# GpSimd's large elementwise work to VectorE, and a planner's matmul cost set to the traced spacing

## The chip, the cores and the metric

The kernel runs on one core of a Trainium2 chip. The metric is the device time of one execution in microseconds (us). TensorE does the products, ScalarE, VectorE and GpSimd the elementwise work, and SyncE (SP) issues the loads.

## The reference, cut to what matters

Two transformer blocks on 256 tokens of 1024 features, in 32-bit floats, one after the other:

```
x = x + 0.5 * rms_norm(swiglu(rms_norm(x)))            # ffn1
x = x + rms_norm(mixer1(rms_norm(x)))                  # windowed attention, window means
x = x + 0.5 * rms_norm(swiglu(rms_norm(x)))            # ffn2
x = x + concat(ssd(u), mla(u)) @ w_out_2               # second mixer: recurrence and latent attention
x = x + memory_attention(rmsnorm(x), rmsnorm(mem))
x = x + conv_ffn(rmsnorm(x))                           # taps along the tokens
return rmsnorm(x)
```

The feed-forward width is 2816; every weight is used once for the 256 tokens.

## The kernel before

**Split products.** To keep 32-bit accuracy each operand is split in two parts of a shorter format: `hi` is the rounded value, `lo` the rest. A product is three matmuls, `hi*hi + hi*lo + lo*hi`, summed in one bank of PSUM (`mm3`, `mm2`, `projB`). The other products (transposes, scores, recurrence) are in plain 32-bit floats.

**Weights.** `wblock` (L660) loads up to 1024 columns on 128 partitions into one of four `raw` tiles, ScalarE copies them into `hi`, and a subtraction gives `lo`. The raw tile is free again when the subtraction has ended. Which engine subtracts is set in `sub` (L600): always VectorE in the phases "start", "ffn" and "cffn", VectorE or GpSimd in "mix" (first mixer) and "mix2" (second mixer and the attention over the memory), by the table `POOL_LO` (L30).

**Products of two tiles.** `mul` (L597) may run on VectorE or GpSimd in every phase. It scales the attention weights (`softmax_p` with `norm`), makes the decays and scaled inputs of the recurrence (`ssd_rec`), the scaled tokens (`Into.done`) and the last gains (`Final.half`).

**Small work.** The norms' power of -0.5 on one column is always on GpSimd (`rsq`, `rstd`). `copy` and `scale` may run on ScalarE or VectorE.

**Order.** `Plan` records every instruction with its tiles, its allowed engines and an estimated time (`Plan.cost`, L280). `Plan.schedule` (L304) is a list schedule: again and again it takes, of all engines, the instruction that can start first, with the earlier recorded one first among equals. Where two engines are allowed, one that would finish later than the other has the difference added to its start. Tiles get slots, and a load or write waits for a slot. The instructions are then issued in the order of their planned starts (L470 issues all, so the profile gives this line for nearly everything). On each engine that order is fixed: an instruction that has to wait holds all that follow it on its engine.

The estimates in question:

```
if dt == F32R:                                                        # L288
    return 2.5 + (n / 2.4 if n >= 256 else 4 * n / 2.4)               # one matmul of n columns, ns
...
return (0.52 if one else 1.04) * size(out) + (130 if ps else 70)      # VectorE
return 1.05 * size(out) * (2 if out.tile.dtype == F32R else 1) + 464  # GpSimd
```

For 1024 columns with the split's output type the planner puts a subtraction at 1135 ns on VectorE and 2614 ns on GpSimd. It has no cost for one engine slowing another.

Of the kernel before, what the change touches and what calls it, by code (L numbers as in the profile page):

```python
# [9 lines left out]
F32 = mybir.dt.float32  # L10
# [4 lines left out]
ALU = mybir.AluOpType  # L15
# [14 lines left out]
POOL_LO = {"start": 0, "ffn": 0, "mix": 1, "mix2": 1, "cffn": 0}  # L30
# [42 lines left out]
# vectors over features, a chunk of 128 to a column; ffn1_pre apart  # L73
# [3 lines left out]
# short vectors, on every partition  # L77
ROWS = ["sinks", "ssd_dt_bias_2", "ssd_a_log_2", "ssd_d_2"]

# weights, cut by columns: first column, width of a block; a block lies by its row in a chunk of 128, then by chunk  # L80
# [9 lines left out]
def layout(inputs):  # L90
    """the arrays in memory: small vectors packed, the others as they are"""
    out = dict(inputs)
    cols = lambda name: np.asarray(out.pop(name)).reshape(-1, P).T
    c = constants()
    out["first"] = cols("ffn1_pre")
    out["cols"] = np.concatenate([cols(n) for n in COLS], axis=1)
    out["rows"] = np.concatenate([np.asarray(out.pop(n)).reshape(1, -1) for n in ROWS], axis=1)
    out["pos"] = np.concatenate([cols("positions"), cols("positions_2")], axis=1)
    out["xT"] = np.asarray(out["x"])[0].reshape(2 * P, KD, P).transpose(2, 1, 0)
    for name, cuts in TILED.items():  # L100
        w = np.asarray(out.pop(name))[0]
        for (c0, n), (c1, _) in zip(cuts, cuts[1:] + [(w.shape[1], 0)]):
            out[f"{name}_from{c0}"] = w[:, c0:c1].reshape(-1, P, (c1 - c0) // n, n).transpose(2, 1, 0, 3)
    return {**out, **c}


class Tile:
    """A tile on chip before it has an address: taken from a class of slots at its first write."""
# [16 lines left out]
class View:  # L125
    """Slices of a tile, kept until the tile has an address; ix tells which columns they touch, rows which partitions."""
# [85 lines left out]
class Plan:  # L212
    """Records the instructions of the program, orders them on their engines by a list schedule that follows
    their data, their slots and their estimated times, and then issues them to Tile in that order."""
# [40 lines left out]
    def access(self, n, v, w):  # L255
        t = v.tile
        if t not in n.tiles:
            assert w or t.acc, ("read before any write", n.label)
            n.tiles.append(t)
            t.left += 1  # L260
        if t.cls == "ps":
            mask, rows = np.ones(1, bool), (0, P)
        else:
            mask, rows = np.zeros(int(np.prod(t.shape[1:])), bool), v.rows
            mask[v.ix[0].ravel()] = True
        keep = []
        for m, ow, omask, orows in t.acc:
            if m is not n:
                hit = rows[0] < orows[1] and orows[0] < rows[1] and (omask & mask).any()
                if hit and (w or ow):  # L270
                    n.deps.add(m)
                # a write that covers an earlier access takes its place
                if w and rows[0] <= orows[0] and orows[1] <= rows[1] and not (omask & ~mask).any():
                    continue
            keep.append((m, ow, omask, orows))
        keep.append((n, w, mask, rows))
        t.acc = keep

    @staticmethod
    def cost(attr, op, a, k):  # L280
        out = k.get("out", a[0] if a else None)
        size = lambda v: int(np.prod(v.shape[1:]))
        ps = any(isinstance(v, View) and v.tile.cls == "ps" for v in list(a) + list(k.values()))
        if attr == "tensor":
            if op == "transpose":
                return 109.0
            n, dt = size(out), k["rhs"].tile.dtype
            if dt == F32R:  # L288
                return 2.5 + (n / 2.4 if n >= 256 else 4 * n / 2.4)
            return 5 + max(n, P) / 2.4 * (4 if dt == F32 else 1)  # L290
        if attr == "sync" or op == "dma_start":
            n = int(np.prod(out.shape)) * 4
# [3 lines left out]
        if attr == "vector":  # L296
            if op == "reduce_max":
                return 1.04 * size(a[1]) + 70
            one = op in ("tensor_copy", "tensor_scalar") and not ps
# [4 lines left out]
    def schedule(self):  # L304
# [9 lines left out]
        known = {e: [] for e in names}  # L314
# [9 lines left out]
        weights = 0  # L324
# [12 lines left out]
        def slot_time(n):  # L337
            """when the slots of the node's new tiles are there; None: not yet known"""
# [5 lines left out]
            for c, ts in need.items():  # L344
# [10 lines left out]
                # the oldest tiles keep the last slots, and none runs far ahead of them  # L355
# [117 lines left out]
class Transposed:  # L473
    """Chunks of 128 features of one tile of tokens, split in two; four chunks of both tiles of tokens to a tile of memory."""
# [13 lines left out]
class Into:  # L488
    """The tokens transposed and split for the products that follow. late: not scaled, their products are; rows: and
    with the scales along the tokens; both: and scaled as well."""  # L490
# [49 lines left out]
class Final:  # L540
    """The last norm, and out."""
# [24 lines left out]
class K:  # L566
# [23 lines left out]
    def transposed(self, nk):  # L590
        """memory for nk chunks of both tiles of tokens"""
        return tuple([self.w1024(F32R) for _ in range(0, nk, 4)] for _ in range(2))
# [4 lines left out]
    def mul(self, out, a, b):  # L597
        self.nc.add([(e, "tensor_tensor", (out, a, b), {"op": ALU.mult}) for e in ("vector", "gpsimd")])

    def sub(self, out, a, b):  # L600
        alts = ["vector"] + ["gpsimd"] * POOL_LO[self.phase]
        self.nc.add([(e, "tensor_sub", (out, a, b), {}) for e in alts])
# [29 lines left out]
    def load_xT(self, k0, k1):  # L632
        """chunks of the tokens as they lie transposed, with their gains, split"""
# [20 lines left out]
    def bc(self, v, ap):  # L654
        """one row on every partition"""
        self.nc.sync.dma_start(v, ap.partition_broadcast(P))
        return v

# [1 line left out]
    def wblock(self, src):  # L660
# [8 lines left out]
        sub = (lo[:, :n], raw[:, :n], hi.bitcast(F32)[:, :n])  # L669
        self.sub(*sub)  # L670
# [36 lines left out]
    def mm2(self, ps, a, b, sa, sb, start, stop):  # L707
        """one chunk of the product of two split operands"""
# [6 lines left out]
    def rsq(self, ss, e):  # L715
        """the sum of two sums of squares and e, and its -0.5th power"""
# [11 lines left out]
    def rstd(self, src, n, ce=1.0):  # L728
        """(mean square of n columns + ce * eps) ** -0.5"""
# [7 lines left out]
    def to_T(self, src, xT, k0, gain=None, n=4, keep=None):  # L737
        """n chunks of src (tokens by n*128) transposed into chunks k0.. of xT"""
# [18 lines left out]
    def residual(self, t, h, ps, post=None):  # L757
        """post: scale of the row and gains"""
# [12 lines left out]
    def down(self, name, w, lhs, nxt, post=None, blocks=None):  # L771
        """tokens by 1024, added to x; lhs[t] lists (row chunk of w, transposed operand, chunk in it); post: gains, factor and, where the
        rows are so many times too small, squares of the divisors, of a norm before; the second tile runs lag blocks behind; yields after each block"""
# [52 lines left out]
    def ffn(self, name, src, nxt, side=None, first=None):  # L826
        """features with the tokens along; the gates are scaled, the others stay unscaled, up to the norm behind; first: at
        the start, what reads the tokens; else the first 512 features token tile by token tile"""
# [19 lines left out]
        for f0 in range(0, KF, 2) if first else (0, *range(4, KF, 2)):  # L848
# [31 lines left out]
            if f0 == 0:  # L880
                # a bank to a product: they take turns over the rows of their weights
# [16 lines left out]
    def rope_tables(self):  # L898
# [30 lines left out]
        # per tile: [cos cos | -sin sin] for 8 and for 16 frequencies  # L929
# [9 lines left out]
    def apply_rope(self, v, t, o, n):  # L939
        """v: tokens by heads by 2n, rotated in place"""  # L940
# [13 lines left out]
    def mixer1(self, xT, nxt):  # L954
# [65 lines left out]
        for t in range(2):  # L1020
# [3 lines left out]
            # windowed attention with sinks  # L1024
# [29 lines left out]
            # causal window means  # L1054
# [25 lines left out]
    def projB(self, ps, w, f, xT, k0=0, k1=None):  # L1080
        """features f*128.. of the block's columns by 256 tokens"""
# [10 lines left out]
    def conv(self, out, ps, bias, w, taps):  # L1092
        """causal taps along the tokens of one chunk of features, and the bias; w(j): the tap of column j"""
# [5 lines left out]
    def softplus(self, out, v, n):  # L1099
        """max(v, 0) + log(1 + exp(-|v|))"""  # L1100
# [22 lines left out]
    def softmax_p(self, sc, nh, W, sinks=None, scale=None, split=False, norm=False):  # L1123
        """exp of nh rows' scores less their maximum, transposed, and one over their sums; 512 columns"""
# [34 lines left out]
    def mixer2(self, xT, nxt):  # L1159
# [21 lines left out]
        # time steps, latents, shared rotary key  # L1181
# [32 lines left out]
        # state inputs and outputs of the recurrence, features by tokens  # L1214
# [22 lines left out]
        # decays  # L1237
# [21 lines left out]
        def mla_proj(g):  # L1259
            """queries, keys and values of four heads"""  # L1260
# [30 lines left out]
        def mla_attn(g, kT, vt, qT):  # L1291
            self.label(f"mla attn{g}")
            for t in range(2):
                W = P * (1 + t)
                nh = 512 // W
                for h0 in range(0, 4, nh):
# [6 lines left out]
                    # the values of two heads times the weights of both: a head's own half of the rows is its output  # L1303
# [10 lines left out]
        def ssd_x(g):  # L1314
            """the recurrence's inputs of four heads, tokens by features"""
# [18 lines left out]
        def ssd_z(g):  # L1334
            """twice the gate of half the heads"""
# [14 lines left out]
        def ssd_rec(g):  # L1350
            """the recurrence of four heads"""
# [3 lines left out]
            for t in range(2):  # L1355
# [4 lines left out]
                # decays between tokens times the products of their states  # L1360
# [84 lines left out]
    def memory(self, xT, nxt):  # L1445
# [4 lines left out]
        def heads(label, w, x):  # L1450
            """features by 256 rows, split, a head to 512 columns"""
# [52 lines left out]
    def conv_ffn(self, out):  # L1504
# [4 lines left out]
        for f0 in range(0, KF, 2):  # L1509
# [7 lines left out]
            if f0 == 0:  # L1517
                # on the tokens not yet scaled, the half of their features that comes first ahead
# [103 lines left out]
```

## Time and profile before

| | |
|---|---|
| timed runs | 1017.09 us median of 3 (1016.87 to 1021.49) |
| span of the profiled execution | 1026.3 us; no other time of it is given |
| TensorE (PE) busy | 985.9 us, 96% |
| VectorE (DVE) busy | 699.1 us, 68%, 1123 instructions |
| ScalarE (ACT) busy | 516.3 us, 50% |
| GpSimd (POOL) busy | 183.3 us, 18%, 134 instructions |
| moved by DMA | 167.48 MB, mean 163 GB/s |

The span runs from the first to the last instruction of one execution. Busy shares are means over stages with different limits: what a change is worth is read from the stage in which it acts, and from what ends the waits there. TensorE's instructions overlap in the engine, so its busy time says where it waited rather than how well it was used. The stages, in us from the span's start: ffn1 to about 180, first mixer to 285, ffn2 to 462, second mixer to 720, attention over the memory to about 830, the convolving feed forward to the end.

### The profile page before, as it was taken

How to read it: one execution, taken by the hardware profiler on the slowest of the kernel's cores; microseconds unless marked ns; L12 is line 12 of the kernel's file. 1: busy time of each engine (PE TensorE's matmuls, PEld its weight loads, DVE VectorE, ACT ScalarE, POOL GpSimd, SP SyncE). 2: the span in 40 equal slices, each digit the busy share in tenths (PEclk: the TensorE clock that was granted, in tenths of full speed). 3: DMA queues.
4: the chain of work that ended last, by engine and by line, in shares of the span. 5: the costliest groups of instructions: out<-in, count | busy, mean ns of one | idle time of the engine just before them, and what ended most of it. 6: DMA issues, size and time to landing. Idle time of an engine off the chain costs nothing.

```text
span 1026.3 us, 16435 instructions
## 1 busy us (share of the span) xinstructions
PE 985.9 (96%) x6437; PEld 891.5 (87%) x6437; DVE 699.1 (68%) x1123; ACT 516.3 (50%) x842; POOL 183.3 (18%) x134
## 2 busy tenths in 40 slices
PE   8999999999999999999898999987999999999997
PEld 7999988877889999887887888766998889999885
DVE  5786534576586656346998788998714788888552
ACT  5665333365365433334665776463544357656331
POOL 0000000230000000004452243664463020000001
PEclk9999999996899999999999999999999999999999
DMA  7876544663158555454452543123755056656351
GB/s 256 275 268 226 170 139 144 233 208 103 42 159 285 172 164 167 141 174 147 144 180 94 166 129 139 42 82 130 240 187 164 30 195 207 205 189 203 122 164 41
DMA packets 49421, 167.48 MB, mean 163 GB/s; under 512 B 5824, under 2 KB 7360, under 8 KB 49344
## 3 DMA queue, kind: packets, MB, share of 16 engines
q1 hardware_dynamic: 49344, 166.44, 50.2%
q8 instruction: 50, 0.82, 0.3%
q14 instruction: 27, 0.22, 0.1%
HBM read 165.37 MB, written 1.05 MB: 162 GB/s over the span
## 4 chain that ended last, share of the span: by engine, by line
PE 75%; DVE 13%; DMA 5%; issue 3%; ACT 3%; SPq 0%; POOL 0%; POOLq 0%; DVEq 0%; ACTq 0%
PE t L470 75%; DVE t L470 13%; ACT t L470 3%; DMA t<-in_w_in_from_dram 2%; DMA t<-in_ffn_w_gu_from_dram 2%; DMA t<-in_w_out_from_dram 1%; DMA t<-in_xT_dram 1%; DMA t<-in_w_ffn_up_from_dram 0%; SPq L470 0%; ACT L470 0%; POOL t L470 0%; POOLq L1618 0%; DVEq L470 0%; ACTq L470 0%; POOLq L470 0%
## 5 line engine op out<-in xcount | busy, mean ns | idle before, releaser
L470 PE MATMUL t<-t,t 128*128 128x256 f32 (+7 forms) x6428 | 981.9, 316 | 32.5 <-DVE t L470 24.2
L470 PEld LDWEIGHTS t<-t,t 128*128 128x128 f32 (+1 forms) x6412 | 889.2, 189 | 123.7 <-DVE t L470 21.0
L470 DVE TENSOR_TENSOR t<-t,t 128x1024 fp32r<-128x1024 f32 (+13 forms) x710 | 550.7, 813 | 270.6 <-PE t L470 118.8
L470 ACT CAST t<-t 128x1024 fp32r<-128x1024 f32 (+7 forms) x406 | 358.1, 900 | 309.8 <-PE t L470 162.8
L470 POOL TENSOR_TENSOR t<-t,t 128x1024 fp32r<-128x1024 f32 (+6 forms) x120 | 180.9, 1520 | 833.3 <-DVE t L470 677.4
L470 ACT ACTIVATE t<-t 128x512 f32<-128x512 f32 (+9 forms) x132 | 73.4, 558 | 137.2 <-DVE t L470 92.0
L470 ACT ACTIVATE t<-t,t 128x256 f32<-128x256 f32 (+4 forms) x139 | 67.1, 513 | 33.1 <-DVE t L470 15.6
L470 DVE SCALAR_TENSOR_TENSOR t<-t,t,t 128x254 f32<-128x254 f32 (+5 forms) x158 | 68.6, 492 | 20.0 <-ACT t L470 14.7
L470 DVE CAST t<-t 128x512 fp32r<-128x512 f32 (+9 forms) x55 | 25.9, 474 | 7.1 <-PE t L470 5.9
L470 ACT COPY t<-t 128x256 f32<-128x256 f32 (+3 forms) x34 | 14.8, 447 | 22.7 <-PE t L470 22.7
L470 DVE TENSOR_SCALAR t<-t,t 128x128 f32<-128x128 f32 (+9 forms) x37 | 15.0, 420 | 9.9 <-POOL t L470 4.0
L470 DVE TENSOR_SCALAR t<-t 128x1 f32<-128x1 f32 (+4 forms) x69 | 14.2, 218 | 5.2 <-ACT t L470 2.5
L470 DVE TENSOR_REDUCE t<-t 128x2 f32<-128x512 f32 (+1 forms) x22 | 14.9, 684 | 1.6 <-PE t L470 1.6
L470 DVE SCALAR_TENSOR_TENSOR t<-t,t 128x512 f32<-128x512 f32 (+2 forms) x17 | 13.3, 782 | 3.2 <-ACT t L470 2.9
L470 DVE COPY t<-t 128x256 f32<-128x256 f32 (+5 forms) x27 | 13.1, 485 | 3.2 <-PE t L470 3.2
L470 ACT ACTIVATION_READ_ACCUMULATOR t<-t 128x1 f32 x60 | 11.4, 189 | 0.0
L470 ACT ACTIVATION_READ_ACCUMULATOR t<-t,t 128x1 f32 x48 | 10.1, 210 | 0.0
L470 ACT ACT_TABLE_LOAD x7 | 9.0, 1283 | 1.3 <-PEq L1610 0.7
L470 PEld LDWEIGHTS <-t 128*128 128x128 bf16 x25 | 2.4, 119 | 4.0 <-issue 2.4
L470 ACT ACTIVATE t<-t,t,t 128x256 f32<-128x256 f32 x8 | 4.4, 560 | 2.3 <-DVE t L470 2.3
L470 DVE RECIPROCAL t<-t 128x2 f32<-128x2 f32 (+2 forms) x23 | 4.0, 172 | 1.8 <-ACT t L470 1.5
L470 PE MATMUL t<-t 128*128 128x512 bf16 x9 | 4.0, 631 | 1.2 <-DVE t L470 1.2
(10 smaller groups left out, 5.4 us busy)
## 6 DMA issues: line engine op xcount, KB each, us to landing
t<-in_ffn_w_gu_from_dram SPq DMA_DIRECT2D x85, 512.0 KB, 4.8
t<-in_ffn_w_down_from_dram SPq DMA_DIRECT2D x44, 512.0 KB, 4.0
t<-in_w_ffn_up_from_dram SPq DMA_DIRECT2D x44, 512.0 KB, 4.6
t<-in_w_in_from_dram SPq DMA_DIRECT2D x34, 512.0 KB, 4.3
t<-in_w_out_from_dram SPq DMA_DIRECT2D x24, 512.0 KB, 4.5
t<-in_w_ffn_down_from_dram SPq DMA_DIRECT2D x22, 512.0 KB, 4.5
t<-in_w_mem_k_from_dram SPq DMA_DIRECT2D x8, 512.0 KB, 3.9
t<-in_w_mem_q_from_dram SPq DMA_DIRECT2D x8, 512.0 KB, 5.1
```

The costliest lines, as they stand in the source:

```text
L470: getattr(getattr(nc, attr), op)(*[real(v) for v in a], **{x: real(v) for x, v in k.items()})
```

## The change

Three edits. The table `POOL_LO` and the function `sub` go, and every weight's subtraction is VectorE's. `mul` is VectorE's alone. The planner's time of a one-pass matmul becomes 4.0 + 0.4453 n ns: 118.0 instead of 109.2 ns for 256 columns, 232.0 instead of 215.8 ns for 512. GpSimd keeps the powers of one column, two small copies and the fills with ones. The diff also takes out the comments and docstrings, which alters no instruction.

```diff
-POOL_LO = {"start": 0, "ffn": 0, "mix": 1, "mix2": 1, "cffn": 0}
...
             if dt == F32R:
-                return 2.5 + (n / 2.4 if n >= 256 else 4 * n / 2.4)
+                return 4.0 + (0.4453 * n if n >= 256 else 4 * n / 2.4)
...
     def mul(self, out, a, b):
-        self.nc.add([(e, "tensor_tensor", (out, a, b), {"op": ALU.mult}) for e in ("vector", "gpsimd")])
-
-    def sub(self, out, a, b):
-        alts = ["vector"] + ["gpsimd"] * POOL_LO[self.phase]
-        self.nc.add([(e, "tensor_sub", (out, a, b), {}) for e in alts])
+        self.nc.vector.tensor_tensor(out, a, b, op=ALU.mult)
...
         nc.scalar.copy(hi[:, :n], raw[:, :n])
-        sub = (lo[:, :n], raw[:, :n], hi.bitcast(F32)[:, :n])
-        self.sub(*sub)
+        nc.vector.tensor_sub(lo[:, :n], raw[:, :n], hi.bitcast(F32)[:, :n])
```

## Rows read from the trace of the kernel before

**Rows 1.** The page's chain that ended last: shares of the span by engine.
```profile
PE 75%; DVE 13%; DMA 5%; issue 3%; ACT 3%; SPq 0%; POOL 0%; POOLq 0%; DVEq 0%; ACTq 0%
```

**Rows 2.** Busy time by stage: stretch, length, busy us (instructions), granted clock, DMA.
```profile
180.00:285.00 105.00, 100.86 (x516) 84.19 (x515) 64.23 (x124) 51.53 (x108) 19.53 (x16) 0.89 0.43 143
462.00:590.00 128.00, 116.83 (x731) 105.82 (x729) 107.12 (x220) 75.90 (x158) 46.52 (x29) 0.97 0.46 147
590.00:720.00 130.00, 117.86 (x684) 99.19 (x683) 114.56 (x204) 73.73 (x164) 63.70 (x51) 0.99 0.33 106
720.00:850.00 130.00, 128.13 (x883) 117.83 (x882) 75.49 (x111) 63.09 (x93) 45.12 (x21) 1.00 0.49 158
```
The busy columns are TensorE's matmuls (PE), its weight loads (PEld), VectorE, ScalarE and GpSimd.

**Rows 3.** TensorE's timeline, 462 to 720: start, us, [idle before <- who ended it].
```profile
537.15 1.83 PE L470 MATMUL t<-t,t 128*128 128x128 f32 x8 [1.42 <-DVE t L470]
543.02 43.67 PE L470 MATMUL t<-t,t 128*98 128x128 f32 x266 [4.04 <-DVE t L470]
...
603.81 10.97 PE L470 MATMUL t<-t,t 128*128 128x128 f32 x66 [1.28 <-DVE t L470]
...
690.20 2.92 PE L470 MATMUL t<-t,t 128*128 128x128 f32 x16 [1.32 <-DVE t L470]
694.47 5.02 PE L470 MATMUL t<-t,t 128*128 128x128 f32 x25 [1.35 <-DVE t L470]
702.11 14.23 PE L470 MATMUL t<-t,t 128*128 128x128 f32 x58 [2.63 <-DVE t L470]
717.81 107.35 PE L470 MATMUL t<-t,t 128*128 128x128 f32 x720 [1.46 <-DVE t L470]
```

**Rows 4.** Timelines of VectorE and of GpSimd, 528 to 543.
```profile
528.65 0.68 DVE L470 SCALAR_TENSOR_TENSOR t<-t,t 128x512 f32<-128x512 f32 x1
...
534.36 2.73 DVE L470 SCALAR_TENSOR_TENSOR t<-t,t 128x512 f32<-128x512 f32 x1
...
533.93 7.77 POOL L470 TENSOR_TENSOR t<-t,t 128x1024 fp32r<-128x1024 f32 x3 [6.11 <-ACT t L470]
```

**Rows 5.** GpSimd's groups by shape, 462 to 720: count, busy us, mean ns, idle before.
```profile
L470 POOL TENSOR_TENSOR t<-t,t 128x1024 fp32r<-128x1024 f32 x21 | 52.9, 2534 | 53.2 <-ACT t L470 28.8 <-PE t L470 24.3
L470 POOL TENSOR_TENSOR t<-t,t 128x512 fp32r<-128x512 f32 x12 | 14.4, 1210 | 9.7 <-DVE t L470 5.9 <-PE t L470 3.8
...
L470 POOL TENSOR_TENSOR t<-t,t 128x256 f32<-128x256 f32 x13 | 10.7, 827 | 0.3 <-PE t L470 0.3
```

**Rows 6.** VectorE's largest groups by shape, 462 to 720.
```profile
L470 DVE TENSOR_TENSOR t<-t,t 128x1024 fp32r<-128x1024 f32 x29 | 37.1, 1301 | 2.4 <-ACT t L470 2.2
L470 DVE TENSOR_TENSOR t<-t,t 128x512 f32<-128x512 f32 x37 | 30.7, 839 | 5.2 <-PE t L470 4.4 <-ACT t L470 0.2
L470 DVE TENSOR_TENSOR t<-t,t 128x512 fp32r<-128x512 f32 x30 | 29.2, 985 | 3.4 <-ACT t L470 1.7 <-PE t L470 1.4
```

**Rows 7.** VectorE's groups by shape, 285 to 462, beside no large GpSimd work.
```profile
L470 DVE TENSOR_TENSOR t<-t,t 128x1024 fp32r<-128x1024 f32 x62 | 74.8, 1222 | 53.0 <-PE t L470 18.0 <-issue 17.9 <-ACT t L470 17.1
...
L470 DVE TENSOR_TENSOR t<-t,t 128x512 fp32r<-128x512 f32 x15 | 10.2, 690 | 2.0 <-PE t L470 1.0 <-ACT t L470 0.8
```

**Rows 8.** Waits: us in total, times, longest; 180 to 285, then 462 to 590.
```profile
PE t L470 <- POOL t L470: 1.0, 2, 0.6
...
POOL t L470 <- ACT t L470: 48.1, 8, 25.5
```

**Rows 9.** Busy time in two stretches that hold products only, columns as above.
```profile
154.00:180.00 26.00, 26.00 (x114) 21.13 (x113) 12.38 (x11) 9.18 (x11) 0.00 (x0) 1.00 0.48 142
359.00:385.00 26.00, 26.00 (x222) 26.00 (x221) 15.05 (x17) 9.75 (x11) 0.00 (x0) 1.00 0.51 163
```

**Rows 10.** Busy time in two stretches with a lower granted clock, columns as above.
```profile
239.00:263.00 24.00, 23.90 (x101) 20.67 (x102) 12.19 (x38) 11.78 (x41) 1.10 (x2) 0.51 0.10 32
539.00:565.00 26.00, 21.98 (x130) 19.79 (x131) 20.48 (x56) 13.38 (x39) 5.08 (x3) 0.93 0.27 91
```

**Rows 11.** TensorE's timeline in the first mixer.
```profile
239.10 46.17 PE L470 MATMUL t<-t,t 128*128 128x128 f32 x223 [1.23 <-ACT t L470]
```

## The prediction

> **What bounds the kernel now.** I read first the page's chain of work that ended last: TensorE holds 75% of the span, VectorE 13%, GpSimd 0% [rows 1]. So only what makes TensorE wait, or run slowly, can move the time. Next I read the busy time by stage [rows 2]. GpSimd does its large work in four stretches, and TensorE's own loss differs between them: 105.00 - 100.86 = 4.1 us in the first mixer (180 to 285), 128.00 - 116.83 = 11.2 us and 130.00 - 117.86 = 12.1 us in the two halves of the second mixer (462 to 720), 130.00 - 128.13 = 1.9 us in the attention over the memory (720 to 850). The second mixer loses 23.3 us and is the place to look.
>
> There I read TensorE's timeline. Seven of its waits there, all ended by VectorE, add up to 1.42 + 4.04 + 1.28 + 1.32 + 1.35 + 2.63 + 1.46 = 13.5 us [rows 3]. Why VectorE was late is in its own timeline. A SCALAR_TENSOR_TENSOR of 512 columns takes 0.68 us at 528.65 and 2.73 us at 534.36. GpSimd started three subtractions of 1024 columns at 533.93 and spent 7.77 us, 2.59 us each, so the first ended near 536.5 and the slow VectorE instruction at 537.1 [rows 4]. VectorE stood still while GpSimd worked, and 543.02, TensorE's longest wait, stands right behind this. All seven waits have a VectorE instruction of this kind, stretched to 2.2 to 2.9 us beside a GpSimd subtraction, within the 6 us before them. So GpSimd's help costs VectorE time that the planner does not know of: it puts a GpSimd subtraction at 2.6 us and charges VectorE nothing.
>
> **The change part by part.**
>
> **Work moved.** In 462 to 720 GpSimd runs 21 subtractions of 1024 columns (2.53 us each), 12 products of 512 (1.21) and 13 of 256 (0.83), and 12 more of 384 to 768 columns [rows 5]. On VectorE undisturbed, 1024 columns take 1.222 us and 512 take 0.690 us [rows 7]. So VectorE gets 21 x 1.222 = 25.7, 12 x 0.69 = 8.3, 13 x 0.41 = 5.4 (an estimate: half of GpSimd's 0.83, as with 1024 columns), and about 10 for the last twelve (14.7 at most, at 1.222 each): 49 us.
>
> **Time given back to VectorE.** The same shapes are slower in this stretch than in 285 to 462, where GpSimd has no large work [rows 6, 7]: 29 x (1.301 - 1.222) = 2.3, 37 x (0.839 - 0.690) = 5.5, 30 x (0.985 - 0.690) = 8.9, together 16.7 us. These three groups hold 97.0 of VectorE's 107.12 + 114.56 = 221.7 us [rows 2, 6]; if the others lose in proportion it is 38.2 us. The ends are 16.7 (others lose nothing) and 78.0 (every microsecond of the three GpSimd groups blocks [rows 5]); I take 38, because the small shapes are blocked for as long as the large ones. VectorE's load rises by 49 - 38 = 11 us against 258 - 221.7 = 36 us of idle time: it does not become the bound by its sum.
>
> **What TensorE gets.** The seven waits lose their cause. In its place an instruction that TensorE needs may find a subtraction running on VectorE: at most 1.22 us, on the mean 0.61, seven times 4.3 us. So **-9.2 us**; the ends are -13.5 (no subtraction in the way) and the loss of the second rival below.
>
> **Clock.** The granted clock is 0.93 over 539 to 565, behind the wait of 4.04 us [rows 10], and there is one more stretch like it behind the wait at 702. Each costs at most 0.07 x 26 = 1.8 us. Shorter waits should save half: **-1.8**, ends 0 and -3.6.
>
> **First mixer.** Five subtractions. TensorE waited for GpSimd itself 1.0 us in two waits [rows 8]. **-0.5**; ends -1.0, and +2.4 if two VectorE subtractions of 1.22 us come in front.
>
> **Memory attention.** GpSimd's 45.12 us go to VectorE as about half, 22 us, where VectorE is busy 75.49 of 130 us and TensorE waits for nearly nothing [rows 2]. **0**; what hides it is VectorE's 54 us of idle time. If that cover failed, the split weights of the products would be late next, by one subtraction, +1.2.
>
> **Elsewhere** the subtractions were on VectorE already. The powers of one column stay on GpSimd. No DMA is added or moved, but a raw weight tile comes free when its subtraction ends, now in VectorE's order, and SP's queue holds the next load until then.
>
> **The estimate.** It changes no instruction's work, only the plan: the order, and the engine of those copies and scalings that ScalarE or VectorE may run. In pure product stretches 26.00 us hold 222 matmuls, most of them of 256 columns, and 114 of 512 [rows 9]: 117.1 and 228 ns. The old cost gives 109.2 and 215.8 ns, the new 118.0 and 232.0. The new one is nearer. With it the plan sees TensorE some 8% slower, and puts splits of weights ahead of evacuations more often. TensorE's losses that the seven waits do not explain, 23.3 - 13.5 = 9.8 us in the second mixer and 3.1 in the first, are all that a better order could win; half of it, 6.5, is my end on either side, and I take **0**, since nothing in the trace says which way a new order falls.
>
> The Trainium skill's page TensorE: Matmul & The Clock Gate, section "Wait — 56ns, not 53.3ns?", gives N / 2.4 GHz plus about 2.5 ns between warm matmuls, which is the old cost to the digit. By it the new cost would be the wrong one, the plan would be 8% too slow for TensorE, and this term would go to its bad end; the trace does not agree (117.1 and 228 ns), so I leave the term as it is. The bad end alone, 1005.6 + 6.5, is 1012 us; I give that course 0.02, inside the case of no change below.
>
> **Sum.** -9.2 - 1.8 - 0.5 = -11.5 us on the profiled span of 1026.3. That execution has no other time; the timed runs' median, 1017.1, lies 9.2 us (0.9%) below the span. I carry the difference over unchanged: 1017.1 - 11.5 = 1005.6, so **1006 us**, 1.1% faster.
>
> **The rivals.**
>
> **No change.** VectorE is busy 114.56 of 130 us in the second half [rows 2], and what is given back (38, perhaps 17) may be less than what is added (49). Then TensorE's waits stay, with subtractions as their cause. For it: the near balance. Against it: the subtractions are half as long and the plan now knows them. It also covers an estimate that alters nothing that matters. 1012 to 1022, middle 1017.
>
> **Slower: a split that waits holds VectorE's queue.** GpSimd waited 48.1 us, in 8 waits, for ScalarE's copy in 462 to 590 [rows 8]. There it held only further splits. In VectorE's queue, worked off in order, every evacuation behind such a split waits too, and TensorE with it. If 40% of it, 19.2 us, reaches TensorE, the time is 1017.1 - 11.5 + 19.2 = 1025. It decides from 11.5 / 48.1 = 24% on. Against it: the plan places splits by when the copy should be done.
>
> **Much faster: the half clock of the first mixer goes too.** From 239 to 263 the granted clock is 0.51, that is, nearly all at 1.2 GHz [rows 10]; just before, TensorE waited 1.23 us for ScalarE [rows 11]. If it stays at 2.4 GHz, 24 x 0.49 = 11.8 us more are won: 994. Against it: TensorE is busy 23.90 of those 24 us and the clock still did not rise, so the small 4-byte products there, not waits, may keep it low. The Trainium skill's same page, Part 1 ("What's actually happening"), says that the gate follows how busy TensorE has been; by that rule a denser first mixer would hold the full clock, and the busy share in that row speaks against it.
>
> **How the numbers follow.** Forecast 0.53, range 998 to 1012; no change 0.24; slower 0.15; much faster 0.08. About 0.5%, 5.1 us, is what a measurement of this kernel can tell from no change. Faster by more: 0.53 + 0.08 = 0.61; within: 0.24; slower: 0.15. The range from 995 to 1022 leaves out most of the last two cases.
>
> **What would show it.** Right: GpSimd's busy time in the four stretches falls to what its powers take; no VectorE instruction of 512 columns above 1.3 us; means in 462 to 720 fall to those of 285 to 462; TensorE's loss in the second mixer falls from 23 to about 13 us. Wrong: the loss stays and VectorE's waits for ScalarE grow there (the slower rival), VectorE is busy all through the second mixer (no change), or the time moves with a stretch of half clock.

## The result, and the profile after

The changed kernel takes 1004.95 us (median of 10 runs, 1001.89 to 1015.94). The kernel before, timed beside it on the same chip, takes 1018.69 (10 runs, 1016.87 to 1026.8). The ratio is 0.9871, 95% interval 0.983 to 0.9912: 13.7 us or 1.3% faster.

The profiled execution of after took 1004.54 us with a span of 1002.8, so 1.7 us lie outside the span. With the same 1.7 (an estimate) the execution of before with its span of 1026.3 took some 1028 us, above all ten of its runs here. The two spans therefore differ by 23.5 us where the runs differ by 13.7. The excess is mostly one stretch, shown further down: half clock from 239 to 263 us [rows 10]. TensorE's busy time differs by 985.9 - 974.9 = 11.0 us, and the time in which it stands idle by 12.5 (1026.3 - 985.9 = 40.4 us in before, 27.9 in after). A lower clock comes and goes between executions of one kernel: 19 others of before, timed beside later experiments, fall into 13 of 1015.48 to 1021.15 us at a mean granted clock of 0.991 to 0.994, and six of 1026.25 to 1030.32 us at 0.982 to 0.985; the profiled one has 0.982.

The page of after, busy times and chain that ended last:

```profile
PE 974.9 (97%) x6437; PEld 882.1 (88%) x6437; DVE 710.4 (71%) x1201; ACT 519.6 (52%) x846; POOL 38.9 (4%) x52
...
PE 75%; DVE 9%; DMA 7%; ACT 4%; issue 3%; POOL 1%; SPq 0%; POOLq 0%; ACTq 0%; DVEq 0%
```

GpSimd falls from 183.3 to 38.9 us, VectorE rises from 699.1 to 710.4: 144 us of GpSimd's work cost VectorE 11. On the chain VectorE has 9% instead of 13% [rows 1].

Busy time by stage of after, columns as in rows 2:

```profile
180.00:285.00 105.00, 102.20 (x558) 84.44 (x558) 72.91 (x140) 57.76 (x119) 6.82 (x12) 0.98 0.47 159
...
462.00:590.00 128.00, 124.68 (x829) 113.35 (x828) 119.14 (x266) 86.97 (x178) 9.98 (x9) 1.00 0.47 149
590.00:720.00 130.00, 123.98 (x740) 107.66 (x739) 116.80 (x234) 77.55 (x162) 12.76 (x13) 0.97 0.42 138
720.00:850.00 130.00, 128.00 (x894) 118.33 (x894) 92.15 (x138) 68.69 (x103) 2.72 (x2) 1.00 0.51 166
```

In the second mixer (the middle two rows) TensorE loses 3.3 + 6.0 = 9.3 us instead of 23.3, though VectorE is busier: 235.9 instead of 221.7 us of 258. In the first mixer it loses 2.8 instead of 4.1. In the attention over the memory it loses 2.0 as before, with VectorE at 92 instead of 75 us. The stretches are equal in time and not quite in work: from 462 to 720 TensorE does 1567 matmuls in after, 1412 in before.

TensorE's waits for VectorE and VectorE's for ScalarE (us in total, times, longest) in 462 to 720, before and after:

```profile
DVE t L470 <- ACT t L470: 22.2, 27, 5.5
PE t L470 <- DVE t L470: 19.0, 15, 4.0
```
```profile
DVE t L469 <- ACT t L469: 11.8, 21, 3.5
...
PE t L469 <- DVE t L469: 4.7, 8, 1.3
```

VectorE's largest groups by shape in after, 462 to 720, which answer to rows 6:

```profile
L469 DVE TENSOR_TENSOR t<-t,t 128x1024 fp32r<-128x1024 f32 x59 | 71.0, 1217 | 1.5 <-ACT t L469 1.4
L469 DVE TENSOR_TENSOR t<-t,t 128x512 fp32r<-128x512 f32 x47 | 31.6, 686 | 5.5 <-ACT t L469 5.1 <-PE t L469 0.3
L469 DVE TENSOR_TENSOR t<-t,t 128x512 f32<-128x512 f32 x44 | 29.5, 687 | 4.8 <-PE t L469 4.0 <-ACT t L469 0.4
```

1301 has become 1217 ns, 985 has become 686 and 839 has become 687: the values that rows 7 show away from GpSimd's large work. What got slower is GpSimd's own: its two copies of 128 columns (292 ns in before, 1154 in after) and its powers of one column:

```profile
L469 POOL TENSOR_TENSOR t<-t,t 128x1 f32<-128x1 f32 x19 | 20.3, 1069 | 218.9 <-DVE t L469 218.9
```

The same 19 in before (its GpSimd groups of this stretch):

```profile
L470 POOL TENSOR_TENSOR t<-t,t 128x1 f32<-128x1 f32 x19 | 12.5, 660 | 209.2 <-DVE t L470 209.2
```

The longest of them makes TensorE's longest remaining wait in this stretch. Timelines of VectorE, GpSimd, ScalarE and TensorE in after:

```profile
677.89 4.23 DVE L469 TENSOR_TENSOR t<-t,t 128x512 fp32r<-128x512 f32 x6
...
679.39 3.13 POOL L469 TENSOR_TENSOR t<-t,t 128x1 f32<-128x1 f32 x1 [5.36 <-DVE t L469]
...
682.56 1.34 ACT L469 ACTIVATE t<-t,t 128x512 f32<-128x512 f32 x2 [2.88 <-POOL t L469]
...
683.34 36.89 PE L469 MATMUL t<-t,t 128*128 128x128 f32 x246 [2.23 <-ACT t L469]
```

Six subtractions stand back to back on VectorE until 682.12. The power, 0.55 us at 1008.93 in before with nothing beside it, starts at 679.39 and ends only at 682.52, behind the last of the six. ScalarE waits for it, and TensorE for ScalarE.

### The profile page after: what moved, and what is told of

It is laid out like the page before. It is cut to its first block, busy times and chain, and to the rows that moved or that the text cites. A ratio compares the mean times of both kernels' runs of the same rounds, so it can differ in the third digit from the quotient of the medians.

```text
span 1002.8 us, 16342 instructions
## 1 busy us (share of the span) xinstructions
PE 974.9 (97%) x6437; PEld 882.1 (88%) x6437; DVE 710.4 (71%) x1201; ACT 519.6 (52%) x846; POOL 38.9 (4%) x52
## 4 chain that ended last, share of the span: by engine, by line
PE 75%; DVE 9%; DMA 7%; ACT 4%; issue 3%; POOL 1%; SPq 0%; POOLq 0%; ACTq 0%; DVEq 0%
PE t L469 75%; DVE t L469 9%; ACT t L469 4%; DMA t<-in_w_in_from_dram 3%; DMA t<-in_ffn_w_gu_from_dram 2%; POOL t L469 1%; DMA t<-in_w_out_from_dram 1%; DMA t<-in_xT_dram 1%; SPq L469 0%; DMA t<-in_mla_w_kv_up_from_dram 0%; ACT L469 0%; POOLq L1612 0%; ACTq L469 0%; DVEq L469 0%; POOLq L469 0%
## 5 line engine op out<-in xcount | busy, mean ns | idle before, releaser
L469 PE MATMUL t<-t,t 128*128 128x256 f32 (+6 forms) x6428 | 971.4, 314 | 19.9 <-DVE t L469 11.2
L469 PEld LDWEIGHTS t<-t,t 128*128 128x128 f32 (+2 forms) x6412 | 880.0, 187 | 109.9 <-DVE t L469 16.4
L469 DVE TENSOR_TENSOR t<-t,t 128x1024 fp32r<-128x1024 f32 (+13 forms) x792 | 581.7, 777 | 240.6 <-PE t L469 121.2
L469 ACT CAST t<-t 128x1024 fp32r<-128x1024 f32 (+5 forms) x406 | 359.9, 903 | 313.1 <-PE t L469 146.6
L469 ACT ACTIVATE t<-t 128x512 bf16<-128x512 f32 (+10 forms) x132 | 72.8, 557 | 126.1 <-DVE t L469 88.7
L469 POOL TENSOR_TENSOR t<-t,t 128x1 f32<-128x1 f32 x38 | 33.4, 879 | 954.7 <-DVE t L469 954.7
L469 DVE TENSOR_SCALAR t<-t,t 128x128 f32<-128x128 f32 (+7 forms) x33 | 10.1, 317 | 14.0 <-POOL t L469 4.5
L469 DVE TENSOR_SCALAR t<-t 128x1 f32<-128x1 f32 (+5 forms) x69 | 10.1, 157 | 4.1 <-ACT t L469 2.9
L469 DVE SCALAR_TENSOR_TENSOR t<-t,t 128x512 f32<-128x512 f32 (+2 forms) x17 | 9.2, 544 | 0.6 <-ACT t L469 0.4
L469 POOL COPY t<-t 128x8 f32<-128x8 f32 (+1 forms) x6 | 4.7, 810 | 4.2 <-DMA t<-in_cst_dram 3.8
```

Of the source, the lines that this page charges most:

```text
L469: getattr(getattr(nc, attr), op)(*[real(v) for v in a], **{x: real(v) for x, v in k.items()})
```

## The experiments

The ratios are to the kernel before, timed beside each on the same chip. **Theory** (the prediction's): GpSimd's large work stops VectorE, and the gain is in the move. **Rivals**: the gain is in the planner's new cost; or it is nothing but an order that fell well.

**The move alone**, with the old cost:

```diff
-                return 4.0 + (0.4453 * n if n >= 256 else 4 * n / 2.4)
+                return 2.5 + (n / 2.4 if n >= 256 else 4 * n / 2.4)
```

> All large subtractions and products on VectorE, the planner's matmul cost as before. Theory (GpSimd's work stops VectorE, and its removal is the whole gain): 0.985 to 0.992 of the kernel before, and VectorE's means in 462 to 720 fall to 1.22 us (1024 columns) and 0.69 us (512). Rival (the new matmul cost orders the queues better and is the gain): 0.996 or slower, because VectorE then only carries more work.

Measured: 1004.98 us (1002.26 to 1014.88), ratio 0.9876 (0.9824 to 0.9928). VectorE's means in 462 to 720 are 1215 ns (1024 columns) and 685 (512), as the theory had. The move is the whole gain; beside it the new cost is worth nothing that these runs can tell.

**The cost alone**: the kernel before, the diff above the other way round.

> The planner's matmul cost as after the change, GpSimd keeps its large work. Theory: 0.997 to 1.003 of the kernel before, VectorE's stretched instructions remain. Rival (the cost is the gain): 0.987 to 0.993. A third view, that any new order moves the time by several microseconds either way, expects 0.993 to 1.007 with the stretched instructions in place.

Measured: 1047.1 us, ratio 1.0294 (1.0236 to 1.0351). Slower, which none of the three views had. Busy time of this kernel in the second mixer, and GpSimd's group on its page:

```profile
462.00:720.00 258.00, 224.30 (x1334) 197.42 (x1333) 213.04 (x401) 145.25 (x317) 117.39 (x83) 0.93 0.35 112
```
```profile
L470 POOL TENSOR_TENSOR t<-t,t 128x1024 fp32r<-128x1024 f32 (+5 forms) x131 | 206.4, 1592 | 826.1 <-DVE t L470 657.0
```

TensorE loses 258.0 - 224.3 = 33.7 us here instead of 23.3, its waits for VectorE are 30.9 us in 18 instead of 19.0 in 15, and the clock is 0.93. Less the 38 powers, GpSimd runs 93 large instructions instead of 82 (before's page has 120 in this group). What stands beside them may count as well. VectorE's and GpSimd's timelines of this kernel:

```profile
525.25 0.18 DVE L470 TENSOR_TENSOR t<-t,t 128x32 f32<-128x32 f32 x1
...
525.68 2.37 DVE L470 TENSOR_TENSOR t<-t,t 128x32 f32<-128x32 f32 x1
528.08 2.25 DVE L470 TENSOR_SCALAR t<-t 128x32 f32<-128x32 f32 x1
530.37 0.19 DVE L470 TENSOR_TENSOR t<-t,t 128x32 f32<-128x32 f32 x1
```
```profile
525.60 4.69 POOL L470 TENSOR_TENSOR t<-t,t 128x1024 fp32r<-128x1024 f32 x2 [2.08 <-ACT t L470]
```

Two instructions of 32 columns, 0.18 us each otherwise, take 2.37 and 2.25 us: as long as one GpSimd subtraction each. In rows 4 the same happened to an instruction of 512 columns, 2.73 instead of 0.68 us. So in these rows a block adds about the length of GpSimd's instruction, for 32 columns as for 512, and an order that puts GpSimd's subtractions beside a chain of small VectorE instructions should pay most. That this makes up the 30 us is argued, not shown.

**Subtractions alone to VectorE** (the products may still run on GpSimd, new cost), and **products alone** (the subtractions may):

```diff
-POOL_LO = {"start": 0, "ffn": 0, "mix": 1, "mix2": 1, "cffn": 0}
+POOL_LO = {"start": 0, "ffn": 0, "mix": 0, "mix2": 0, "cffn": 0}
```

> The weights' subtractions on VectorE and the new cost; products may still run on GpSimd. Theory: most of the gain, 0.987 to 0.992, since 45 of some 82 large GpSimd operations go, the longest ones. Rival (the products of the recurrence, which stand on a chain, are what counts): 0.995 or slower.

```diff
-        self.nc.add([(e, "tensor_tensor", (out, a, b), {"op": ALU.mult}) for e in ("vector", "gpsimd")])
+        self.nc.vector.tensor_tensor(out, a, b, op=ALU.mult)
```

> The products on VectorE and the new cost; weights' subtractions may still run on GpSimd. Theory: 0.995 to 1.0, since the subtractions of 2.5 us each still stop VectorE. Rival (the products count): 0.987 to 0.992.

Measured: subtractions alone 1005.22 us, ratio 0.9883 (0.983 to 0.9936); products alone 1061.12, ratio 1.0437 (1.0375 to 1.0498). The subtractions are the whole gain, though GpSimd is still busy 58.6 us in the second mixer, some 41 of them with products. VectorE's groups there, with the subtractions alone moved:

```profile
L470 DVE TENSOR_TENSOR t<-t,t 128x512 f32<-128x512 f32 x35 | 28.4, 822 | 5.1 <-PE t L470 4.2 <-ACT t L470 0.3
...
L470 DVE TENSOR_TENSOR t<-t,t 128x256 f32<-128x256 f32 x37 | 18.3, 522 | 0.1
```

These take 822 ns instead of 687, and 522 instead of 419 in after: the products slow VectorE too. But they take work from it (228.3 us busy instead of 235.9), and TensorE waits for it hardly more (6.4 us in 13).

Moving the products while the subtractions stay is worse than the cost alone (1.0437 against 1.0294, intervals apart), which neither expectation had. GpSimd has about as many subtractions of 1024 columns in the second mixer, 24 against 23. TensorE's waits for VectorE there, and the small group that is stretched most:

```profile
PE t L470 <- DVE t L470: 36.0, 14, 7.7
```
```profile
L470 DVE TENSOR_TENSOR t<-t,t 128x64 f32<-128x64 f32 x16 | 13.6, 887 | 0.0
```

The same 16 instructions take 218 ns in after, 241 in before and 618 with the cost alone, while VectorE's subtractions of 1024 columns here, at 1222 ns, are not stretched at all. This fits the chain of small instructions above; no run changes that order alone.

**Work on GpSimd that nobody needs.** To show the block without a change of what VectorE has to do, GpSimd subtracts each second weight block of the second mixer and the memory attention from itself into a spare tile that is never read. The spare tile takes one slot, so the control is after with that slot gone.

```diff
+SLOTS = {"w": 34, "raw": 4, "s": 14, "tiny": 24, "ps": 8}
```

> The kernel after the change with 34 instead of 35 slots for tiles of 1024 columns: the control of the next run, which needs the room. Both theories: 0.985 to 0.995 of the kernel before.

```diff
+        self.nb += 1
+        if self.phase == "mix2" and self.nb % 2:
+            nc.gpsimd.tensor_sub(self.waste[:, :n], hi.bitcast(F32)[:, :n], hi.bitcast(F32)[:, :n])
```

> As the control, and GpSimd subtracts beside every second block of weights from the second mixer's start on, into a tile that nobody reads; the output is the reference's, and VectorE's work is as after the change. Theory (GpSimd's large operations stop VectorE, whoever needs their result): some 45 operations of 2.5 us, 110 us of GpSimd; at the 0.34 us of VectorE that each GpSimd microsecond cost in the kernel before, VectorE loses 35 to 40 us, and the time grows by 8 to 25 us over the control. Rival (the gain came from the shorter subtractions and the order of the queues, not from VectorE being stopped): within 3 us of the control.

Measured: control 1005.22 us, ratio 0.9806 (0.9729 to 0.9883), a little under what was expected; with the unused work 1029.73, ratio 1.0086 (1.0046 to 1.0127). That is 24.5 us by the medians, at the upper end of what was expected, and 28.5 by the ratios, above it. (The ratios are not the quotients of the medians. Before had 1018.77 here, so the quotients are 0.9867 and 1.0108, and for the two runs after these 1.0165 and 1.0030.) The page, VectorE's groups in 462 to 720 and TensorE's wait there, with the unused work:

```profile
L469 POOL TENSOR_TENSOR t<-t 128x1024 fp32r<-128x1024 f32 (+3 forms) x46 | 99.0, 2152 | 153.3 <-ACT t L469 153.1
```
```profile
L469 DVE TENSOR_TENSOR t<-t,t 128x1024 fp32r<-128x1024 f32 x48 | 64.1, 1346 | 4.3 <-PE t L469 3.0 <-ACT t L469 1.3
L469 DVE TENSOR_TENSOR t<-t,t 128x512 fp32r<-128x512 f32 x42 | 31.0, 752 | 0.5 <-ACT t L469 0.3
...
PE t L469 <- DVE t L469: 21.1, 18, 3.2
```

VectorE has the same work as in the control and takes 1346 ns instead of 1216 and 752 instead of 685; TensorE waits 21.1 us for it instead of 4.8. These 16.3 us are most of the 18.6 that TensorE stands idle longer in this stretch (258.0 - 230.3 = 27.7 instead of 258.0 - 248.9 = 9.1). VectorE's busy time over the whole run grows from 708.7 to 745.7 us, 0.37 us for each microsecond of the 99.0. Two other things can be a part of the 24.5 us: the unused instruction holds its `hi` tile longer, and GpSimd's powers queue behind it (ScalarE waits for GpSimd 16.0 us in 8 instead of 9.1 in 6).

**How far the cost matters.** The kernel before with a cost half way between old and new (113.6 ns for 256 columns), and after with a cost as far again above the new one (126.8 ns):

```diff
-                return 2.5 + (n / 2.4 if n >= 256 else 4 * n / 2.4)
+                return 3.25 + (0.431 * n if n >= 256 else 4 * n / 2.4)
```

> The kernel before, with a matmul cost halfway between the old and the new one (113.6 and 223.9 ns). If the new cost is harmful in itself while GpSimd has its large work, this lies between: 1.01 to 1.02 of the kernel before. If any new order only throws the dice anew on which VectorE instructions stand beside GpSimd's runs, it may fall anywhere from 0.99 to 1.04, not in the order of the costs.

```diff
-                return 4.0 + (0.4453 * n if n >= 256 else 4 * n / 2.4)
+                return 5.5 + (0.474 * n if n >= 256 else 4 * n / 2.4)
```

> The kernel after the change with a matmul cost as far above the new one as that is above the old (126.8 and 248.2 ns). If the cost matters only while GpSimd's large work is there: 0.984 to 0.991 of the kernel before, as with either of the other costs. If a wrong cost harms by itself: 0.995 or more.

Measured: 1035.6 us, ratio 1.0116 (1.0047 to 1.0186), and 1021.79, ratio 1.0002 (0.996 to 1.0043). With GpSimd's subtractions in place the time rises with the cost: 1, 1.0116, 1.0294. Three points can stand in order by chance, so the other view is not ruled out. Without them 109 and 118 ns are equal and 127 ns takes the whole gain back. There TensorE loses 7.4 + 8.7 = 16.1 us in the second mixer, against 9.3 in after, and waits 10.7 us for VectorE (14 waits) against 4.7 (8). Its busy time by stage:

```profile
462.00:590.00 128.00, 120.58 (x791) 108.64 (x790) 110.32 (x250) 83.24 (x169) 10.14 (x10) 1.00 0.44 138
590.00:720.00 130.00, 121.35 (x707) 101.64 (x706) 121.34 (x246) 75.57 (x163) 11.13 (x13) 1.00 0.40 131
```

So with the subtractions on VectorE none of the three costs does better than the traced one, and the too high one costs as much as GpSimd's help did; with them on GpSimd the old cost is the best of three. By which step of the schedule, these runs don't show.

**What is left, and a better version.** If VectorE still binds the second mixer, copies that are free to go to ScalarE should help (`tk`, `kT` and the transposed queries of the latent attention through `copy`); if the loads bind it, a fifth `raw` tile should (with 34 slots, so that it fits); if the reach ahead of the splits binds it, a higher cap should; and the first and the last were put together.

```diff
-                nc.vector.tensor_copy(tk[:, :, :64], kv[:, :, :64])
+                self.copy(tk[:, :, :64], kv[:, :, :64])
```

> The kernel after the change; the copies of the latent attention's keys out of PSUM (8 of 256 columns, 8 of 98 x 512, some 9 us of VectorE) and of its queries may run on ScalarE or VectorE. If VectorE's load now bounds the second mixer (119 and 117 of 128 and 130 us busy): 3 to 7 us faster than after the change, 0.980 to 0.985 of the kernel before. If late weights or the norms' powers on GpSimd bound it: within 2 us of after the change, 0.985 to 0.989.

```diff
-SLOTS = {"w": 35, "raw": 4, "s": 14, "tiny": 24, "ps": 8}
+SLOTS = {"w": 34, "raw": 5, "s": 14, "tiny": 24, "ps": 8}
```

> The kernel after the change with 5 instead of 4 tiles for weights as loaded (and 34 slots for the large tiles, as in the control e5). If weights that come late, their load held until a subtraction on VectorE frees a tile, bound the second mixer (DMA 8% of its chain): 3 to 8 us faster than after the change. If VectorE's load bounds it: no faster, 0.985 to 0.990 of the kernel before, since the subtractions wait on VectorE all the same.

```diff
-CAP = {"start": 22, "ffn": 22, "mix": 16, "mix2": 16, "cffn": 22}
+CAP = {"start": 22, "ffn": 22, "mix": 16, "mix2": 20, "cffn": 22}
```

> The kernel after the change with up to 20 instead of 16 tiles of split weights held at once in the second mixer. Late weights: 2 to 6 us faster than after the change. VectorE's load: within 2 us. A plan's order that is as good as any: up to 5 us either way.

> The free copies and the 20 tiles together. If they mend different things (VectorE's load, and TensorE's reach ahead): 0.970 to 0.976 of the kernel before, some 992 us. If both mend the same one: as the better of the two, 0.976 to 0.980.

Measured: free copies 1000.36 us, ratio 0.9813 (0.9763 to 0.9863); fifth tile 1005.25, 0.9863 (0.9817 to 0.9909); cap of 20 997.06, **0.9776** (0.9733 to 0.982); copies and cap 998.93, 0.9827 (0.9799 to 0.9855). The fifth tile brings nothing that these runs can tell, so a lack of raw tiles does not bind (loads hold 7% of after's chain). The free copies came out as forecast for VectorE's load, but their interval overlaps that of after, and TensorE's waits for VectorE in the second mixer did not fall (6.2 us in 8, against 4.7 in 8): that VectorE's load binds is not shown. The cap gives the best median of all, 2.2% below before and 7.9 us below after, more than any view expected. Its interval and that of after (0.983 to 0.9912) just fail to meet, and all its runs (995.31 to 999.81) lie under all of after's, but the two were not timed side by side: the gain over before is shown, that over after likely. Its row for 590 to 720, against 123.98 us of TensorE in after:

```profile
590.00:720.00 130.00, 127.28 (x792) 110.51 (x792) 118.48 (x230) 77.16 (x160) 10.40 (x13) 1.00 0.46 148
```

Here TensorE loses 2.7 us instead of 6.0, and the clock is 1.00 instead of 0.97. The two gains do not add up, and the pair missed both ranges forecast for it; whether both mend the same thing or some microseconds of either are the order's luck, these runs don't tell.

## Why the prediction was right

It said 1006 us, range 995 to 1022, faster with 0.61; it came out at 1004.95. The main mechanism is shown and not only argued: the move alone gives the gain, the subtractions alone give it, and unused subtractions put on GpSimd take it away again, most of it in TensorE's waits for VectorE. One of its signs held too: no VectorE instruction of 512 columns takes over 1.3 us in after, where 19 did in before.

That the number came within 1 us is in part luck. The forecast was 11.5 us, the measured change 13.7: the waits gave more than their term and the clock less, and the three runs that the sum started from have a median 1.6 us under that of all ten.

**TensorE's waits, -9.2.** The loss in the second mixer was to fall from 23 to about 13 us; it fell to 9.3, by 14.0 us where the term had 9.2. TensorE's waits for VectorE in 462 to 720 fell from 19.0 us in 15 to 4.7 in 8, by 14.3. The allowance of 0.61 us for each of the seven waits, 4.3 us in all, is about what stands there now (4.7), as a sum; that these are the same waits is not shown. The term was mis-sized because the sum counted only the seven waits over 1.2 us [rows 3], and the small ones went too.

**VectorE's balance, +11.** It was 49 added and 38 given back; VectorE's busy time in this stretch rose by 235.9 - 221.7 = 14.3 us. If 49 were added, some 35 were given back (an estimate, since the stretch holds more work in after). So taking 38, between ends of 17 and 78, fits, and so does the reason given, that small shapes are blocked as long as large ones: the two instructions of 32 columns show it.

**Clock, -1.8.** The stretch at 0.93 behind 539 is gone (1.00 in all of 462 to 590). Two others are at 0.91 in after:

```profile
620.00:640.00 20.00, 17.46 (x94) 14.03 (x94) 18.42 (x44) 10.56 (x28) 0.93 (x2) 0.91 0.26 83
...
680.00:700.00 20.00, 17.77 (x81) 14.48 (x80) 16.17 (x22) 10.56 (x16) 3.93 (x2) 0.91 0.56 183
```

By the clocks of the two halves of the second mixer, 0.03 x 128 + 0.01 x 130 = 5.1 us stood under full clock in before and 0.03 x 130 = 3.9 in after: about 1 us of the 1.8 came (an estimate, from rounded clocks).

**First mixer, -0.5; memory attention, 0.** TensorE's loss fell by 1.3 us in the first, half a microsecond of it forecast, and stayed (1.9 and 2.0) in the second, where VectorE's idle time covered 17 us more.

**The estimate, 0 with ends of 6.5.** The value held, the reason did not. Beside the move the new cost is worth nothing. But 6.5 us as the end on either side bounded it by the losses that a better order could win, and a worse order is not bounded by these. Alone, the new cost made it 2.9% (30 us) slower: the order decides how many subtractions GpSimd takes, and which VectorE instructions stand beside them; that these two make up the 30 us is argued from the rows and not shown. Had the change left the subtractions on GpSimd, the prediction would have been wrong by that.

The Trainium skill's rule in TensorE: Matmul & The Clock Gate, section "Wait — 56ns, not 53.3ns?", is the old cost. The traces of before and after both count 222 matmuls in 359 to 385 (all of 256 columns) and 114 in 154 to 180, which makes 117.1 and 228 ns. The partly covered ones at the ends make these a little small: from start to start the medians there are 118 and 232 ns in before, the new cost. So the rule does not give the spacing here; and the course built on it, 1012 us, did not come, since either cost gives the same time after the move.

**The rivals.** *No change*: VectorE is the busiest engine beside TensorE, 91% of the second mixer, and still TensorE's waits for it fell. *Slower*: subtractions that wait for ScalarE's copy were to hold VectorE's queue. VectorE's waits for ScalarE in 462 to 720 fell instead, from 22.2 us in 27 to 11.8 in 21; so the queue was not held as feared, as the argument against this rival had it. *Much faster*: the half clock of the first mixer. Busy time from 239 to 263, in after and in the control with 34 slots:

```profile
239.00:263.00 24.00, 23.41 (x162) 19.74 (x162) 15.61 (x51) 16.61 (x56) 2.11 (x4) 1.00 0.21 71
```
```profile
239.00:263.00 24.00, 24.00 (x100) 20.15 (x100) 10.04 (x31) 11.09 (x33) 1.09 (x2) 0.51 0.11 39
```

The profiled execution of after has the full clock, that of the control, whose median is the same, has half. The control's profiled execution took 1011.14 us, its three other runs 1002.76 to 1006.82. Runs of before show the same two levels of clock and time (the section on the result). So the stretch belongs to an execution and not to the change, and reading it from one trace as a property of the kernel was the weak point of that rival. It also counted the stretch twice: the timed median that the sum started from lies 9.2 us under the profiled span, about what the stretch costs, so those 11.8 us were no longer there to be won. The prediction's argument against it, that small 4-byte products keep the clock low, falls as well: products of this kind run at full clock in after.

Nor does the busy share in the stretch, or the wait in front of it, tell which clock it gets. The kernel with the move alone:

```profile
239.00:263.00 24.00, 24.00 (x165) 21.02 (x165) 17.36 (x53) 15.04 (x50) 2.53 (x5) 1.00 0.10 33
```

It is busy for 24.00 us at 1.00, the control for 24.00 at 0.51. The wait for ScalarE just before was 0.91 us here and 0.59 in after, where the clock stayed, and 0.69 in the control, where it fell. A full row can also be the low clock's own effect: at 0.51 the control needs 24.00 us for 100 matmuls, at 1.00 after does 162 in 23.41.

The same page's Part 1 ("What's actually happening") has the gate follow how busy TensorE has been. These rows speak against it as the whole story: 24.00 us busy at 0.51, and 24.00 at 1.00.

## What to carry to other kernels

Large elementwise work on GpSimd is not free help beside a busy VectorE: count what VectorE loses for each microsecond of it (here 0.37 us with the unused subtractions), and give a planner that cost or keep the work on VectorE. Time each edit of a change alone: a cost set nearer to the trace made the kernel 2.9% slower until the edit beside it removed what the planner did not know. And compare stages, not spans, of two single executions: 10 us of the spans' difference here was a stretch of half clock that any execution of either may have.

## What was not expected of the hardware

The block works both ways, and a run of VectorE instructions holds GpSimd for more than one of them. The power of one column at 679.39 takes 3.13 us instead of 0.55, over four subtractions of VectorE in a row; the 19 powers of the second mixer take 1069 instead of 660 ns on the mean. The Trainium skill's page SBUF — State Buffer, section "Who interferes with whom", says that GpSimd contends for a shared pair of ports with a VectorE instruction that has two inputs in SBUF (the on-chip memory) or runs in a two-port mode, and that whichever issues first holds the pair for the whole instruction. The trace agrees where GpSimd came first (one small VectorE instruction to each subtraction, 2.37 and 2.25 us), and goes beyond it where VectorE did: GpSimd got no turn between four instructions. What the powers cost in time was not tried: no version without them on GpSimd was run.

It was not expected either that products of GpSimd would do so little harm: some 41 us of them in the second mixer, and the same time as with none, though VectorE's means rise beside them (822 instead of 687 ns). Whether that is because they are shorter (0.76 to 1.62 us there, against 2.53 for a subtraction), because of the work that they take from VectorE, or because of where they stand, no run here tells.
